# The down projection of the sample as seven block products, with its weight sums made by accumulating DRAM transfers in the gates' stage

## The chip, the cores and the metric

The kernel runs on one core of one Trainium2 chip. Its engines work in parallel, each through its own queue of instructions: TensorE (PE, with its weight loads PEld) multiplies matrices into PSUM; VectorE (DVE) and ScalarE (ACT) do elementwise work and copy results out of PSUM; GpSimd (POOL) does some elementwise work and issues part of the transfers; SyncE (SP) issues the rest. An engine takes its queue in order: an instruction that waits holds up all that stand behind it on that engine. The metric is the device time of the whole program in microseconds (us), smaller is better.

## The reference

One layer of a hybrid backbone works on 128 prompt tokens and 512 sample tokens with D = 1024 features, all in 32-bit floats. Mixers with gates and an output projection come first; behind them stands the feed-forward part, which matters here:

```python
def conv_ffn(h, w_up, cw, cb, w_down):
    z = dwconv3(h @ w_up, cw, cb)
    a, g = jnp.split(z, 2, axis=-1)
    return (jax.nn.silu(g) * a) @ w_down

    # in trunk_layer
    h = rmsnorm(x, lw['norm2_g']) * (1.0 + sc2) + sh2
    x = x + g2 * conv_ffn(h, lw['w_up'], lw['ffn_conv_w'], lw['ffn_conv_b'], lw['w_down'])
    # at the end, for the prompt and for the sample
    y = rmsnorm(x, final_norm_g)
```

`w_down` is 2816 x 1024. `g2` is the last of six modulation vectors: the product of silu(c) with 1024 columns of `w_ada`, one for the sample and one for the prompt.

## The kernel before, in words

All large products run in a split form. A 32-bit operand is cut into a high part, which TensorE takes in its fast 32-bit format, and a low part, the rest; a product is high x high + high x low + low x high, three matmuls. The high part is a copy on ScalarE (line 311 for weights, line 1774 for rows), the low part a subtraction on DVE (lines 312 and 1777). So each operand of a product costs both engines a pass.

The program is a list of `units`, one weight tile each with three steps: a load, a split ("prep"), and the matmuls. `ahead(i)` issues the loads of up to four units ahead (`DMA_AHEAD`) and the splits of up to two ahead (`PREP_AHEAD`). Side jobs (generators) are woken by `tick(us)`, which the matmul loops call with planned times; `start` puts such a job on the list and `drain` runs the jobs until something is there. A planner of the language then orders each engine's instructions by its own estimate of what is ready, except those pinned with `keep_in_program_order`; in the gates' and the up projection's stage all of DVE's, ScalarE's and POOL's (`ovec`, `oact`, `opool`) are pinned. Buffers are named regions of SBUF (`region("A", ...)`), used again and again: a region's next writer waits until its last reader is done. `rp` holds three raw weight tiles, `wp` three split ones. PSUM has eight banks, four in pairs (`pg`) and four single (`pm`).

The stages and their place in the profile:

- Up to about 300 us: norm, input projections and mixers, with the first gate tiles.
- 300 to 530 us: the gates (`g_pair`, matmuls at line 1124, branch products at line 1137). Tiles go in 14 pairs, and each pair is computed with seven block products in place of eight, Strassen's scheme in Winograd's form: sums of weight blocks (`g_sums`, DVE) and of operands take the place of one product. Weights come from `w_gp`, two loads of 640 KB per pair (line 1061), a pair ahead. POOL issues one load of branch operands in the third pair and one in the seventh (line 1174).
- 530 to 600 us: output projection (line 1264), second norm. POOL loads x for it (line 1253).
- 600 to 868 us: the up projection (`up_pair`, 22 pairs, matmuls at line 1480), also by seven products; the convolution's taps, the gate and `keep`, which writes one finished tile of 128 features x 641 tokens into the DRAM tensor `actd`, issued by POOL. Its columns are the 512 sample tokens, one pad and the 128 prompt tokens.
- 868 us to the end: the down projection (matmuls at line 1815). This is the stage that is changed.

In the down stage before, the output columns go in two halves `nh` of 512; for each, 11 units of two k (`kk_`, 128 features each) pass. `down_prep` splits the weight tile (128x1024: two k of 512 columns) and two activation tiles of 640 tokens, which `back` has loaded from `actd`. `down_tile` runs, for five row tiles t of 128 tokens (four of the sample, one of the prompt) and two k, three matmuls with the activation as the stationary 128x128 operand and 512 weight columns moving. In the second half the last three units are done together, row tile by row tile, and the prompt's tile is cut into two halves of 256 columns at the very end. `down_out` then multiplies a tile by `g2` (`gained`), adds it to x (`added`), squares and sums it for the norm (ScalarE), multiplies the first half by the norm's weight on POOL, and `down_store` scales and stores it.

Beside this `ada_cols` computes the eight 128-column pieces of `g2` (f = 40 to 47): DVE passes twice over a 128x1024 tile of `w_adt` per piece (line 263). It begins when the up projection is over, and `gain_rows` and `gain_load` turn the result into rows, which the first `down_out` needs.

Of the kernel before, what the change touches and what calls it, by code (L numbers as in the profile page):

```python
# [20 lines left out]
NPAIR = 22  # L21
BRIDGE = 4
# [46 lines left out]
def tile_step(ctx: ExitStack, tc: tile.TileContext, a: dict, outs: list, dbg=None):  # L69
# [168 lines left out]
    def ada_cols(fs, tag, homes, gap, last):  # L238
# [4 lines left out]
        act(cf, cf, AF.Silu)  # L243
# [9 lines left out]
        for f in fs:  # L253
            load(f + 1)
            if f in COLWAIT:
                yield COLWAIT[f]
# [32 lines left out]
    def gain_rows(i):  # L289

        m = pm()
# [664 lines left out]
    hdr = dram.tile([2, 2, P, 4, HC], F32, name="hdr")  # L956

# [382 lines left out]
    actd = dram.tile([NPAIR, P, T + 1], F32, name="actd")  # L1340
# [226 lines left out]
    def keep(p_):  # L1567
        opool.dma_start(actd[p_], up[p_, "z", 1])
# [11 lines left out]
    def up_pair(p_, r):  # L1580
# [30 lines left out]
        elif p_ == NPAIR - 1:  # L1611
            rd[UP + 1] = units[UP + 1][1](ld[UP + 1])
# [4 lines left out]
        if inner:  # L1617
            if p_ + 2 < NPAIR:
                r[p_ + 2] = up_load(p_ + 2)
            elif p_ + 2 == NPAIR:  # L1620
                fx["a01"] = rp.tile([P, 2, T], F32, tag="raw", name=nm("raw"))
                back(fx["a01"], 0, 2)
# [68 lines left out]
    def up_all(_):  # L1691
# [23 lines left out]
        def down_home():  # L1715
            if "col" not in fx:
                fx["col"] = region("X1", [P, 2560])
            return fx["col"][:, 0:D]

        start(ada_cols(range(40, 48), "MG1", lambda f: region("H", [P, D]) if f % 2 else down_home(), 3, 4))  # L1720
# [4 lines left out]
    ag = {}  # L1725
    AGT = ["E", "C", "A", "B", "D"]

    def actk(nh, k):
        if k < 2:
            if nh == 0:  # L1730
                return fx["a01"][:, k]
            if "fn" not in fx:
                fx["fn"] = region("F", [P, 2560])
                back(fx["fn"][:, 0:2 * T].rearrange("p (n t) -> p n t", n=2), 0, 2)
                nc.sync.dma_start(fx["fn"][:, 1280:2304], a["final_norm_g"].partition_broadcast(P))
            return fx["fn"][:, k * T:(k + 1) * T]
        i = (k - 2) // 4
        if i not in ag:
            ag[i] = region(AGT[i], [P, 4, T])
            back(ag[i], 2 + 4 * i, 6 + 4 * i)  # L1740
        return ag[i][:, (k - 2) % 4, :]

    def back(dst, n0, n1):
        src = actd[n0:n1].rearrange("n p t -> p n t")
        nc.sync.dma_start(dst[:, :, 0:TS], src[:, :, 0:TS])
        nc.sync.dma_start(dst[:, :, TS:T], src[:, :, TS + 1:T + 1])


    acc = {}
    x2v = {}  # L1750

# [6 lines left out]

    st3 = const.tile([P, 24], F32, name="st3")

    def down_prep(nh, kk_, pr):
        w = pr()
        if "s" not in fx:
            s_ = region("XH", [P, 4, 2, T], F32R)
            fx["s"] = [s_[:, j] for j in range(4)]
            for i in range(2):
                s_ = region("XL%d" % i, [P, 2, 2, T], F32R)
                fx["s"] += [s_[:, j] for j in range(2)]
        sl = []
        for k in (2 * kk_, 2 * kk_ + 1):  # L1770
            i = (nh * NFF + k) % 8
            s = fx["s"][i]
            hl = [s[:, 0, :], s[:, 1, :]]
            high = act(hl[0], actk(nh, k), AF.Copy)  # L1774
            if nh == 0 and kk_ in (1, 2):
                tc.keep_in_program_order(high)
            vec.tensor_tensor(hl[1], actk(nh, k), hl[0].bitcast(F32), ALU.subtract)
            sl.append(hl)
        return w, sl
# [443 lines left out]
```

## Time and profile before

| | |
|---|---|
| median of three runs | 1022.85 us (1022.79 to 1023.98) |
| span of the profiled execution | 1020.8 us; the page gives no other time for it, so 2.05 us of the median lie around the span |
| TensorE busy | 1008.7 us, 99% |
| DVE, ScalarE, POOL busy | 789.7 us, 538.4 us, 106.1 us |
| DMA | 177.85 MB, 174 GB/s in the mean |
| matmuls of the down stage | 678, from 853.8 to 1013.6 us |
| loads of `w_down` | 22 of 512 KB, 4.2 us to landing in the median |
| writes of `actd` by POOL | 22 of 320.5 KB, 5.5 us to landing |

The rows of the profile read as follows. A group's row gives line, engine, operation, the output and input tiles by name with their shapes, the count, then after the bar the busy time, the mean in ns and the idle time ahead of it with what ended it. A row of windows gives the window, its length, the busy time (and count) of PE, PEld, DVE, ACT and POOL, the granted clock as a share of full speed, the DMA share and GB/s. A row of a timeline or of the chain begins with the start in us and the duration. Matmuls overlap, so the distance from one to the next, not the row's mean, is what one costs. Lines 149 and such are a helper's, behind which many operations stand.

### The profile page before, as it was taken

Reading aid. Unit: us, or ns where it says so; the run is one execution under the profiler, and the core shown is the slowest. Engines: PE = TensorE matmul, PEld = TensorE weight load, DVE = VectorE, ACT = ScalarE, POOL = GpSimd, SP = SyncE. Lnnn points to the kernel's source line nnn. Section 1 sums busy time; section 2 is a strip of 40 time slices with the busy share of each in tenths; the row PEclk is TensorE's granted clock in tenths of the full one; section 3 lists DMA queues with packets and bytes.
Section 4 is the critical chain, followed back from the end, with each engine's and each line's share of the span. In section 5 each row is a group of like instructions: output and inputs, shape, how many; then the busy total and the mean of one; then the engine's idle time right before and its main releaser. Section 6 shows DMA issues by size and latency. Waiting matters only on the chain.

```text
span 1020.8 us, 18766 instructions
## 1 busy us (share of the span) xinstructions
PE 1008.7 (99%) x7572; PEld 953.0 (93%) x7572; DVE 789.7 (77%) x1308; ACT 538.4 (53%) x933; POOL 106.1 (10%) x153
## 2 busy tenths in 40 slices
PE   8999999999999999999999999999999999999997
PEld 6899999999999999999998899999999999888886
DVE  6759899779857676776868879988888887797644
ACT  6642343354545454444544567777777776633432
POOL 1000020322100000000010111111122211001101
PEclk9999999999999999999999999999999999999999
DMA  9864333697562413323288585755555669974212
GB/s 355 322 217 130 126 117 116 168 284 226 120 207 79 155 58 104 136 66 104 61 283 337 212 325 121 198 151 150 150 151 151 157 161 274 363 249 157 83 42 103
DMA packets 55926, 177.85 MB, mean 174 GB/s; under 512 B 8192, under 2 KB 14624, under 8 KB 53280
## 3 DMA queue, kind: packets, MB, share of 16 engines
q1 hardware_dynamic: 45008, 140.60, 40.2%
q0 software_dynamic: 10832, 36.06, 14.7%
q8 instruction: 59, 0.97, 0.4%
q14 instruction: 27, 0.22, 0.1%
HBM read 134.93 MB, written 25.46 MB: 157 GB/s over the span
## 4 chain that ended last, share of the span: by engine, by line
PE 92%; DVE 4%; DMA 2%; ACT 1%; issue 1%; SPq 0%; POOLq 0%; POOL 0%; DVEq 0%; ACTq 0%
PE g L1480 20%; PE m L1124 17%; PE g L363 14%; PE g L1815 8%; PE m L1815 6%; PE g L1137 5%; PE m L1480 4%; PE m L1264 3%; PE g L935 2%; PE g L1264 2%; PE m L149 2%; PE g L149 1%; PE m L1475 1%; PE m L527 1%; DMA A<-in_w_ada_dram 1%
## 5 line engine op out<-in xcount | busy, mean ns | idle before, releaser
L363 PE MATMUL g<-XH,w 128*128 128x320 f32 x704 | 171.0, 317 | 0.1
L363 PEld LDWEIGHTS g<-XH,w 128*128 128x128 f32 x704 | 120.6, 188 | 2.5 <-issue 1.0
L363 PE MATMUL g<-XL,w 128*128 128x320 f32 x352 | 108.7, 309 | 0.0
L363 PEld LDWEIGHTS g<-XL,w 128*128 128x128 f32 x352 | 66.3, 188 | 0.1
L312 DVE TENSOR_TENSOR w<-raw,w 128x1024 fp32r<-128x1024 f32 x34 | 41.5, 1221 | 14.7 <-ACT w L311 9.0
L1124 PE MATMUL m<-XH,w 128*128 128x320 f32 x224 | 52.5, 309 | 0.0
L1815 PE MATMUL g<-w,XH 128*128 128x512 f32 (+1 forms) x216 | 50.2, 385 | 0.0
L1815 PEld LDWEIGHTS g<-w,XH 128*128 128x128 f32 x216 | 39.5, 188 | 8.3 <-ACT XH L1774 0.3
L311 ACT ACTIVATE w<-raw 128x1024 fp32r<-128x1024 f32 x34 | 35.7, 1049 | 21.4 <-PE g L1264 9.9
L1815 PE MATMUL g<-w,XL 128*128 128x512 f32 (+1 forms) x180 | 42.5, 387 | 0.0
L149 DVE SCALAR_TENSOR_TENSOR X<-MG,p2t,X 128x641 f32<-128x641 f32 x44 | 38.9, 884 | 4.3 <-ACT X L149 3.4
L149 DVE SCALAR_TENSOR_TENSOR X<-X,p2t,X 128x641 f32<-128x641 f32 x44 | 38.8, 883 | 1.9 <-ACT X L149 1.0
L1815 PEld LDWEIGHTS g<-w,XL 128*128 128x128 f32 x180 | 33.4, 188 | 7.4 <-DVE dt L1830 0.7
L149 ACT ACTIVATE w<-raw 128x1024 fp32r<-128x1024 f32 (+3 forms) x46 | 38.5, 852 | 2.5 <-DMA raw<-in_w_in_dram 1.4
L1480 PE MATMUL g<-XL,w 128*128 128x320 f32 x240 | 38.6, 310 | 0.0
L1480 PE MATMUL g<-XL,C 128*128 128x320 f32 x240 | 38.4, 309 | 0.0
L1124 PEld LDWEIGHTS m<-XH,w 128*128 128x128 f32 x224 | 38.2, 188 | 0.0
L1480 PEld LDWEIGHTS g<-XL,w 128*128 128x128 f32 x240 | 36.0, 188 | 0.5 <-ACT MG L149 0.3
L1815 PE MATMUL m<-w,XH 128*128 128x512 f32 (+1 forms) x156 | 36.4, 381 | 0.0
L1480 PEld LDWEIGHTS g<-XL,C 128*128 128x128 f32 x240 | 36.0, 188 | 0.4 <-ACT MG L149 0.4
L1124 PE MATMUL m<-XL,w 128*128 128x320 f32 x112 | 34.6, 309 | 0.0
L1815 PEld LDWEIGHTS m<-w,XH 128*128 128x128 f32 x156 | 28.5, 188 | 5.6
(549 smaller groups left out, 2749.8 us busy)
## 6 DMA issues: line engine op xcount, KB each, us to landing
raw<-in_w_up_dram SPq DMA_DIRECT2D x30, 512.0 KB, 5.0
raw<-in_w_gp_dram SPq DMA_DIRECT2D x21, 640.0 KB, 3.9
raw<-in_w_down_dram SPq DMA_DIRECT2D x22, 512.0 KB, 4.2
raw<-in_w_in_dram SPq DMA_DIRECT2D x19, 512.0 KB, 4.3
H<-in_w_adt_dram SPq DMA_DIRECT2D x16, 512.0 KB, 4.2
actd<-X POOLq DMA_DIRECT2D x22, 320.5 KB, 5.5
X<-in_w_adt_dram SPq DMA_DIRECT2D x10, 512.0 KB, 4.3
upd<-XL SPq DMA_DIRECT2D x4, 1280.0 KB, 6.5
```

Of the source, the lines that this page charges most:

```text
L149: r = f(*args, **kw)
L311: act(w[0], raw, AF.Copy)
L312: vec.tensor_tensor(w[1], raw, w[0].bitcast(F32), ALU.subtract)
L363: mm(o, w[:, h, k0 + k, :], r(k)[:, s], start=(k == 0 and i == 0), stop=(k == kt - 1 and i == 2))
L527: mm(m[W * g:W * g + W, (i - s0) * W:(i - s0 + 1) * W], lhs, rhs, start=True, stop=True, tile_position=(64 * par, W * g))
L935: mm(o, x(kx)[:, ts], w[:, h, k, :], start=(kx == 0 and i == 0), stop=(kx == 7 and i == 2))
L1124: mm(o, w[:, k, :], x[:, k, :], start=(first and k == 0 and j == 0), stop=(k == 3 and j == 2), skip_group_check=True)
L1137: mm(pb[:, c, 0:HC], w[:, h + k, :], y[:, x, k, s], start=(k == 0 and j == 0), stop=(k == 1 and j == 2))
L1264: mm(m, mh[k // 2][:, hx, k % 2, t * P:(t + 1) * P], wo[q][:, hw, k % 2, :], start=(k == 0 and i == 0), stop=(k == 7 and i == 2))
L1475: mm(o, w[:, k, :], x[:, k, :], start=(first and not part and k == 0 and j == 0), stop=(part == 1 and k == 3), skip_group_check=True)
L1480: z = mm(o, w[:, k, :], x[:, k, :], start=(first and k == 0 and j == 0), stop=(k == 3 and j == 2), skip_group_check=True)
L1815: mm(ps, sl[k][hx][:, t * P:(t + 1) * P], w[:, hw, k, c0:c1], start=first, stop=end and (last or nh == 1 and t == 4 and kk_ == 7))
```

## The change: what it does

The sample's product (512 tokens x 2816 features by 2816 x 1024) is cut in two in each direction: tokens c = 0, 1 (256 each), features h = 0, 1 (11 tiles of 128 each, `NK`), output columns n = 0, 1 (512 each). The eight block products become seven, in sequence (`PHASES`; the prediction calls them blocks 1 to 7): p = 1, 5, 6, 2, 7, 4, 3. Each has six units: five of two k and one of one k. The prompt's 128 rows keep the plain product: they go along as a third row tile in the four blocks p = 1, 5, 2, 3, and where the weight is a sum (p = 5) the part that is too much is subtracted again.

The weights of p = 5, 6, 7 and 4 are sums of blocks. `down_sums` makes them in DRAM (`wsum`) with 48 transfers of up to 512 KB, 24 plain copies and 24 that add to their destination. POOL issues four of them at the start of each pair of the gates' stage from the second pair on, pinned in its queue. The sums of the operands (p = 5, 6, 7 and 3) are DVE operations of 128x512 in place (`x_sum`), one per unit.

PSUM: the products are accumulated so that later ones add to the banks of earlier ones (`bank`); copies of some banks (`c1`, `u2`, `u3`, `cp`) are kept in SBUF by ScalarE. The upper left, lower right and prompt results are put together in block 6 (`LATER`: `out_22`, `out_11`) from a bank and a copy; POOL multiplies and adds the part of `u2` and `cp` (`taken`), six operations of 128x512. At the end of block 6 come the upper right quarters (`half_two`), and the lower left ones and the prompt's second half with block 7.

`keep` writes in two layouts, one for the sample (`actx`, by feature half and token half) and one for the prompt (`actp`), two transfers where there was one; `x_load` reads them back. The weight loads are 42 in place of 22. There are four w buffers and five raw ones. The pieces of `g2` go on with shorter pauses, from other buffers, and stand still for units 9 to 14 (`PAUSE`); the gain is fetched at unit 26 (`G2`). The first unit's split stands behind the last pair's products in `up_pair`, where it stood ahead of them. `w_down` is laid out on the host as four blocks (`w_dn`).

The diff, cut to its core:

```diff
@@ ada_cols
-        act(cf, cf, AF.Silu)
+        z = act(cf, cf, AF.Silu)
+        if fs[0] == 40:
+            tc.keep_in_program_order(z)
...
             load(f + 1)
+            while R.get("pause"):
+                yield 1
@@ before the gates
+    wsum = dram.tile([4, P, NK, 512], F32, name="wsum")
+    def down_sums():
+        b11, b21, b12, b22 = [a["w_dn"][i] for i in range(4)]
+        s = [wsum[i] for i in range(4)]
+        cuts = [slice(k, min(k + 2, NK)) for k in range(0, NK, 2)]
+        for pairs in (((s[0], b11, 0), (s[2], b22, 0)), ((s[0], b12, 1), (s[2], b12, 1)), ((s[1], s[0], 0),),
+                      ((s[1], b22, 1),), ((s[3], s[1], 0),), ((s[3], b21, 1),)):
+            for k in cuts:
+                for o, i, add in pairs:
+                    if add:
+                        opool.dma_start(o[:, k], i[:, k], accum_op=ALU.add, max_dma_last_dim=1024)
+                    else:
+                        opool.dma_start(o[:, k], i[:, k])
+                    yield
@@ g_all
+        sums_ = down_sums()
         for p_ in range(GPAIR + 1):
+            for _ in range(4 if p_ else 0):
+                next(sums_, None)
@@ keep
-        opool.dma_start(actd[p_], up[p_, "z", 1])
+        z, (h, k) = up[p_, "z", 1], divmod(p_, NK)
+        opool.dma_start(actx[h].rearrange("c p k t -> p c k t")[:, :, k], z[:, 0:TS].rearrange("p (c t) -> p c t", c=2))
+        opool.dma_start(actp[h][:, k], z[:, TS + 1:T + 1])
@@ up_pair
         elif p_ == NPAIR - 1:
-            rd[UP + 1] = units[UP + 1][1](ld[UP + 1])
+            x_load("E")
+            ld[UP + 2] = units[UP + 2][0]()
...
+        if p_ == NPAIR - 1:
+            x_load("C")
+            rd[UP + 1] = units[UP + 1][1](ld[UP + 1])
+            ld[UP + 3] = units[UP + 3][0]()
@@ up_all
-        start(ada_cols(range(40, 48), "MG1", lambda f: region("H", [P, D]) if f % 2 else down_home(), 3, 4))
+        start(ada_cols(range(40, 48), "S0", lambda f: region("H" if f % 2 else "G", [P, D]), 1, 1), 0)
@@ the down stage
+    KS = [(0, 1), (2, 3), (4, 5), (6, 7), (8, 9), (10,)]
+    PHASES = [(1, "w", 0, (0, 0), 0), (5, "s", 0, (0, 1), 0), (6, "s", 1, (0, 0), None), (2, "w", 1, (1, 0), 1),
+              (7, "s", 2, (0, 1), None), (4, "s", 3, (1, 1), None), (3, "w", 3, (1, 0), 1)]
+    DOWN = [(ph, j) for ph in range(7) for j in range(6)]
+    JOIN = {(4, 4), (5, 0), (6, 3), (6, 4)}
...
+    def x_sum(p_, ks):
+        x = lambda h, c: x_raw(h, c, ks)
+        if p_ == 5:
+            vec.tensor_tensor(x(0, 1), x(0, 1), x(1, 1), ALU.subtract)
+        elif p_ == 6:
+            vec.tensor_tensor(x(0, 0), x(0, 1), x(0, 0), ALU.subtract)
+        elif p_ == 7:
+            vec.scalar_tensor_tensor(x(0, 1), x(0, 0), -1.0, x(1, 1), ALU.mult, ALU.subtract)
+        elif p_ == 3:
+            vec.tensor_tensor(x(1, 0), x(1, 0), x(0, 0), ALU.add)
...
+        x_sum(p_, ks)
+        act(w[:, 0, 0:n], raw, AF.Copy)
+        for o, i, r in ((0, 256, x_raw(h, c, ks)),) + (((256, 384, xr["p", hp][:, ks[0]:ks[-1] + 1]),) if hp is not None else ()):
+            act(s[:, 0, 0:n, o:i], r, AF.Copy)
+            vec.tensor_tensor(s[:, 1, 0:n, o:i], r, s[:, 0, 0:n, o:i].bitcast(F32), ALU.subtract)
+        vec.tensor_tensor(w[:, 1, 0:n], raw, w[:, 0, 0:n].bitcast(F32), ALU.subtract)
...
+    def bank(p_, t):
+        if t == 4:
+            return acc["p" if p_ in (1, 2) else "q"]
+        return acc["b3" if p_ == 2 else "b2" if p_ in (5, 3) else "b1"][t]
...
+    def taken(nh, t, x, op):
+        pool.tensor_tensor(x, x, grows["g2"][:, 0 if t < 4 else 1, nh * 512:nh * 512 + 512], ALU.mult)
+        xs = x2[t][:, nh * 512:nh * 512 + 512]
+        pool.tensor_tensor(xs, xs, x, op)
+
+    def half_one(nh, t):
+        xs = x2[t][:, nh * 512:nh * 512 + 512]
+        q = st3[:, t:t + 1]
+        act(prods[t], xs, AF.Square, accum_out=q)
+        pool.tensor_tensor(xs, xs, xr["F"][:, nh * 512:nh * 512 + 512], ALU.mult)
+        vec.tensor_scalar(q, q, 1.0 / D, EPS, ALU.mult, ALU.add)
+
+    def down_out(p_, t, c0, c1, ps):
+        if p_ == 5 and t == 4:
+            vec.tensor_tensor(acc["cp"], ps, acc["cp"], ALU.subtract)
+        elif p_ in (1, 6):
+            act(acc["cp"] if t == 4 else acc["c1" if p_ == 1 else "u2"][t], ps, AF.Copy)
+        elif p_ == 7:
+            act(acc["u3"][t], ps, AF.Copy)
+        elif p_ == 4:
+            half_two(0, t + 2, 0, 512, ps)
+        elif p_ == 3:
+            half_two(1, t, c0, c1, ps)
+
+    def joined(nh, t, ps, x, op):
+        y = gp.tile([P, 512], F32, tag="gt", name=nm("y"))
+        vec.tensor_tensor(y, ps, x, op)
+        gained(nh, t, 0, 512, y)
+        added(nh, t, 0, 512)
+        half_one(nh, t)
...
+    LATER = {(5, 1): (lambda: out_22(0),), (5, 3): (lambda: out_22(1),), (5, 2): (lambda: out_11(0),),
+             (5, 4): (lambda: out_11(1),), (5, 5): (lambda: out_11(4),)}
```

More of the change, by code (lines that the diff above doesn't have):

```diff
@@ L21 @@
 NPAIR = 22
+NK = NPAIR // 2
 BRIDGE = 4
@@ L1757, in x2r @@
         return x2v[tag]
-    st3 = const.tile([P, 24], F32, name="st3")
[L1761 to L1779, printed above, removed]
@@ L1799, in down_tile @@
[L1799 to L1807 removed]
+            x2[4] = x2r("G")[:, 0:1024]
+            r = region("H", [P, 2, 512])
+            acc["u3"] = [r[:, 0], r[:, 1]]
+        for f in LATER.get((ph, j), ()):
+            f()
+    def bank(p_, t):
+        if t == 4:
+            return acc["p" if p_ in (1, 2) else "q"]
+        return acc["b3" if p_ == 2 else "b2" if p_ in (5, 3) else "b1"][t]
@@ L1808, in down_tile @@
+    def down_tile(u, ws):
+        ph, j = DOWN[u]
+        p_, _, _, _, hp = PHASES[ph]
+        down_start(u)
+        hold.append((KS[j], ws))
+        if (ph, j) in JOIN:
+            return
+        batch = hold[:]
+        hold.clear()
+        end = j == 5
+        for t in (0, 1, 4) if hp is not None else (0, 1):
+            halved = p_ == 3 and t == 4 and end
             for ci, (c0, c1) in enumerate(((0, 256), (256, 512)) if halved else ((0, 512),)):
-                ps = (acc["halves"][ci] if halved else acc[nh][t])[:, 0:c1 - c0]
```

210 lines of the change are left out of this document (120 added, 90 removed).

## The prediction

> **What bounds the kernel now.** I read the page's busy shares and its chain of waits first, then windows by stage, then the tables of groups for the last stage alone, and the timeline where two engines meet.
>
> ```profile
> span 1020.8 us, 18766 instructions
> PE 1008.7 (99%) x7572; PEld 953.0 (93%) x7572; DVE 789.7 (77%) x1308; ACT 538.4 (53%) x933; POOL 106.1 (10%) x153
> PE 92%; DVE 4%; DMA 2%; ACT 1%; issue 1%; SPq 0%; POOLq 0%; POOL 0%; DVEq 0%; ACTq 0%
> ```
> ```profile
> 424.00:439.80 15.80, 15.80 (x109) 15.80 (x109) 11.32 (x19) 7.27 (x13) 0.00 (x0) 1.00 0.25 83
> 750.00:800.00 50.00, 50.00 (x343) 50.00 (x342) 44.38 (x65) 35.66 (x62) 9.21 (x12) 1.00 0.60 153
> 900.00:925.00 25.00, 25.00 (x112) 20.67 (x112) 23.33 (x38) 8.29 (x11) 0.00 (x0) 1.00 0.69 233
> 975.00:1000.00 25.00, 25.00 (x112) 20.65 (x111) 10.25 (x13) 6.53 (x9) 0.14 (x1) 1.00 0.07 22
> ```
>
> TensorE never stops in these windows (columns: window, its length, then busy time of PE, PEld, DVE, ACT and POOL, clock, DMA share, GB/s). In the gates (first row) DVE has 4.5 us to spare in each 15.8 and DMA three quarters; in the up projection DVE is at 89%; in the down stage it is at 93% while the last gain columns run and at 41% afterwards. So removed matmul time is time, as long as DVE can feed the shorter stage.
>
> **The matmuls removed.** One row per form, the down stage alone, and the beat of the chain:
>
> ```profile
> L1815 PE MATMUL g<-w,XH 128*128 128x512 f32 x204 | 48.6, 391 | 0.0
> L1815 PE MATMUL g<-w,XL 128*128 128x512 f32 x174 | 41.6, 390 | 0.0
> L1815 PE MATMUL m<-w,XH 128*128 128x512 f32 x144 | 34.8, 389 | 0.0
> L1815 PE MATMUL m<-w,XL 128*128 128x512 f32 x120 | 29.3, 389 | 0.0
> ```
> ```profile
> 877.09 5.44 PE g L1815 x24
> ```
> ```profile
> 1011.60 0.88 PE L1815 MATMUL m<-w,XL 128*128 128x256 f32 x6
> 1012.32 1.60 PE L1815 MATMUL m<-w,XH 128*128 128x256 f32 x12
> ```
>
> 204 + 174 + 144 + 120 = 642 matmuls of 512 columns; the code has 36 more of 256. The beat is 5.44/24 = 0.2267 us, and (1012.32 - 1011.60)/6 = 0.12 us for a half. Before: 642 x 0.2267 + 36 x 0.12 = 149.9 us. After: the sample takes 7 products x 11 k x 2 row tiles x 3 = 462; the prompt, which keeps the plain product, takes 11 x 3 in each of three blocks and, in the last, 18 whole and 30 half ones. That is 579 x 0.2267 + 30 x 0.12 = 134.9 us. **TensorE saves 15.0 us.** Operand shapes stay, so the beat stays.
>
> **What the stage asks of DVE.** The table of groups from 868 us on gives the durations:
>
> ```profile
> L312 DVE TENSOR_TENSOR w<-raw,w 128x1024 fp32r<-128x1024 f32 x20 | 24.4, 1220 | 3.5 <-ACT w L311 3.0
> L1834 DVE TENSOR_TENSOR G<-G,dt 128x512 f32<-128x512 f32 x2 | 1.4, 685 | 0.0
> L1834 DVE TENSOR_TENSOR G<-G,dt 128x256 f32<-128x256 f32 x2 | 0.8, 424 | 0.0
> L1777 DVE TENSOR_TENSOR XH<-E,XH 128x640 fp32r<-128x640 f32 x4 | 3.1, 820 | 4.1 <-ACT XH L1774 4.1
> L1830 DVE TENSOR_TENSOR dt<-g,S 128x512 f32<-128x512 f32 x6 | 4.1, 690 | 6.6 <-PE g L1815 4.6 <-DMA S<-growd 2.0
> L1877 DVE SCALAR_TENSOR_TENSOR X<-X,st,F 128x512 f32<-128x512 f32 x4 | 3.0, 750 | 2.0 <-POOL st L1871 2.0
> L263 DVE SCALAR_TENSOR_TENSOR junk<-H,MG 128x1024 bf16<-128x1024 f32 x4 | 4.9, 1220 | 1.6 <-DMA H<-in_w_adt_dram 1.6
> ```
>
> Neighbours overlap by some 0.08 us, so I count 1.14, 0.61 and 0.35 us for 1024, 512 and 256 columns, and 0.73 where one operation needs the last one's result. Low parts of a unit of two k: weights 1.14, sample rows 0.61, prompt rows 0.35 (four blocks), a sum of operands 0.61 (four blocks). A unit needs:
> - block 1: 2.10 us of DVE against 4.08 of PE (18 matmuls)
> - block 2: 2.71 against 4.08; block 4: 2.10 against 4.08; block 7: 2.71 against 4.08
> - blocks 3 and 5: 2.36 against 2.72 (12 matmuls); block 6: 1.75 against 2.72
>
> The gain columns take two passes of 1.22 us each and some 0.2 for the rest, about 2.6 us, eight times. They run in blocks 1 and 2, stop for units 9 to 14, and end in block 4; blocks 1 and 2 need 5.5 x (2.10 + 2.71) = 26.5 of DVE beside some 17 for six or seven columns, 43.5 of 45 us. That just fits, with weight loads five deep over it. ScalarE, busy 8.3 of 25 us in that window now, has room.
>
> Block 6 is where it does not fit. There the results of four quarters and of the prompt are put together: four joins of three dependent operations (0.73 + 0.73 + 0.61 + 0.15 = 2.2 us), one of 1.5 for the prompt, and after its end two final quarters (0.73 + 0.61 + 0.15 + 0.75 = 2.25 each). From its start to the last low part, with the first two units prepared ahead, DVE has: 3 x 1.75 + 0.95 for units 3 to 6 of the block, 5 x 2.71 + 1.5 for block 7, 8.8 + 1.5 + 4.5 for results, 1.3 for a prompt quarter: 37.3 us. PE has 14.96 + 22.6 us in these two blocks, and the last unit must be ready 7.7 us before the end (its first use comes 10.4 us of matmuls before the end, 2.7 us after that batch's start), which leaves 29.9. DVE can run ahead some 3 us (the w buffers are four, and the first joins read banks that are long done). **Short by 4.4 us**, which PE waits.
>
> **POOL against DVE.** The change adds six POOL multiplications and additions of 128x512 to the five that are there now, all in block 6. This is what one does to DVE now:
>
> ```profile
> L1845 POOL TENSOR_TENSOR X<-X,F 128x512 f32<-128x512 f32 x4 | 5.9, 1485 | 64.2 <-ACT dt L1844 64.2
> ```
> ```profile
> 945.16 1.21 DVE L312 TENSOR_TENSOR w<-raw,w 128x1024 fp32r<-128x1024 f32 x1
> 946.36 1.86 DVE L1777 TENSOR_TENSOR XL<-C,XL 128x640 fp32r<-128x640 f32 x1
> 948.20 2.58 DVE L1777 TENSOR_TENSOR XL<-C,XL 128x640 fp32r<-128x640 f32 x2
> 943.12 1.51 DVE L1834 TENSOR_TENSOR X<-X,dt 128x512 f32<-128x512 f32 x1
> 938.58 0.15 DVE L1846 TENSOR_SCALAR st<-st 128x1 f32<-128x1 f32 x1 [0.79 <-ACT dt L1844]
> 945.47 2.07 POOL L1845 TENSOR_TENSOR X<-X,F 128x512 f32<-128x512 f32 x1 [1.39 <-ACT dt L1844]
> ```
>
> The DVE operation ends at 948.2 instead of 947.2: 1.86 us where the same shape takes 0.82, and POOL's own took 2.07. Three of DVE's were held so (the 1.51 us at 943.12 for 0.68, and one of the pair at 948.20, 2.58 us for 1.55), 2.9 us together for five POOL operations. Eleven would cost 11 x 2.9/5 = 6.4 us; none is the lower end, if DVE happens to read PSUM meanwhile. I take 3, since joins are half PSUM reads and the last POOL operations fall behind the shortage. The stall is then 7.4 us.
>
> The Trainium skill, "SBUF — State Buffer", "Who interferes with whom", says that a VectorE instruction with two SBUF inputs and a GpSimd instruction that reads SBUF share a port and one holds it for its whole length. The rows above agree; taken at its full strength the rule is the second rival below.
>
> **The weight sums in the gates.** 48 transfers of up to 512 KB (23 MB), four per pair from the second pair on. Rows:
>
> ```profile
> L1061 SPq DMA_DIRECT2D raw<-in_w_gp_dram x21: 327/328/383, 267.1 to 475.9; - x21
> DMA to landing us min/median/max: 3.7/3.9/6.2
> 396.73 16.17 SPq L1061 DMA_DIRECT2D raw<-in_w_gp_dram  x3
> 415.89 0.33 SPq L1061 DMA_DIRECT2D G<-in_w_gp_dram  x1
> 421.89 1.35 ACT L149 ACTIVATE w<-raw 128x1024 fp32r<-128x1024 f32 x2
> 343.32 0.57 POOL L1174 DMA_DIRECT2D E<-ybd  x1 [56.82 <-PE g L1137]
> 406.68 0.55 POOL L1174 DMA_DIRECT2D A<-ycd  x1 [62.79 <-PE g L1137]
> 512.61 0.54 POOL L1253 DMA_DIRECT2D G<-in_x_prompt_dram  x1 [105.38 <-DVE D L149]
> L149 POOL DMA_DIRECT2D actd<-X x22 | 18.3, 832 | 19.6 <-DVE X L149 19.6
> q0 software_dynamic: 10832, 36.06, 14.7%
> w<-raw POOLq DMA_DIRECT2D x6, 512.0 KB, 8.2
> ```
>
> POOL has no work there, and nothing paces it but two loads of branch operands (at 343.3 and 406.7 us, both waiting for PE), so the transfers go out in three bursts, of 8, 16 and 24, each beside a few pairs. Queue 0 now moves 36.06 MB in 14.7% of the span, 240 GB/s, so 23 MB are 96 us of transfer time in some 200. An accumulating one has two reads, for which only the 8.2 us of 512 KB into SBUF stand: the last 24 at 8.2 each would run to 406.7 + 197 us and hold back the five loads of x that POOL issues from 512.6 on; at 4 us each they end at 505. They overlap, so I take the shorter. The two weight loads of a pair go out at 412.6 (the last of the three merged in the row) and 415.9 and are first read at 421.9 and, one long split later, 423: 9 and 7 us, of which the landing takes 3.9. ScalarE is busy 7.3 of the pair's 15.8 us, so a late start is partly made up. They may take some 7 to 10 us. I take 0.5 us for this, bounds 0 and 24 (third rival). By "DMA: Bandwidth & Descriptors", "Queues, rings and completion order", in the Trainium skill, engines take queues in turn by packets, by which 3.9 us becomes at most 7.8, and the 0.5 us and the third rival would fall away.
>
> **Small parts.** `keep` issues two transfers instead of one: 22 more of 0.83 us on POOL, which is busy 9.2 of 50 us in that stage; the buffer that they read is written again more than a pair (84 matmuls, 12 us at the windows' 343 in 50) later. SP issues 42 weight loads instead of 22 and waits for the last `keep` before a tail load; five raw buffers cover that. The first unit's split now stands behind pair 21's products instead of ahead of them, so PE has less to fill the end of the up projection with; Silu of the two vectors is pinned on ScalarE behind a 1 MB load. I take 1 us, bounds 0 and 4. The tail keeps its form: two halves of the prompt last.
>
> **Sum.** 1020.8 - 15.0 + 7.4 + 0.5 + 1.0 = 1014.7 us of span; the median of the runs lies 2.05 us above the span, so 1016.8.
>
> **Rivals.**
> 1. *DVE keeps up* (joins and low parts interleave so that PE waits under 3 us). For it: DVE at 93% cost PE nothing from 900 to 925. Against: the 37.3 us above. 1022.85 - 15.0 + 1.5 + 1 = 1010.4.
> 2. *POOL and DVE exclude each other throughout* (slower). If each POOL operation stops DVE for its own 1.28 to 1.49 us, and joins wait for ScalarE's squares as one does for 0.79 us now, block 6 loses 11 x 1.4 = 15 us more: 4.4 + 15 + 1.5, so 1022.85 - 15.0 + 20.9 = 1028.8. It decides from a stall of 13.5 us on. For it: the held operations above waited about as long as POOL's ran. Against: five POOL operations cost DVE only 2.9 us now.
> 3. *The sums hold back the gates' loads.* If a load lands 3 us after its latest time in eight pairs, 24 us in place of the 0.5: 1040.3. For it: a load took 6.2 us where DMA was near full. Against: the 10 us it may take.
> 4. *The saving goes at the borders*, where a bank waits for the copy of its last block: six borders at the 0.8 us that a wait for ScalarE takes above, 5 us on top: 1021.8, no change that can be told.
>
> **Chances.** Mine 0.50, rivals 0.18, 0.17, 0.09 and 0.06. What a measurement can tell is 0.2%, 2 us. Faster: nearly all of the first two, 0.65; same, the edges of mine and the last, 0.12; slower 0.23. Mine alone spans 1012 to 1021; with rival 1 and the near part of rival 2 the range is 1009 to 1028.
>
> **What would show it.** The beat of 0.2267 us with 609 matmuls in the down line; PE without a gap through the first five blocks and gaps released by DVE (low parts of w) in the last two, 4 to 12 us together; DVE over 95% busy there, with 512-column operations of 1.3 us and more beside POOL; pairs of 15.84 us unchanged in the gates. Wrong if the gates' pairs lengthen, if gaps come in the first two blocks (loads or gain columns), or if block 6 runs through.

## The result, and the profile after

The changed kernel takes 1021.82 us (median; 1018.16 to 1025.61), the kernel before, measured beside it, 1022.69 us (1021.96 to 1023.98). The ratio is 0.999, with a 95% interval of 0.9981 to 0.9999: a gain of 0.9 us, where 6 were forecast and 15 us of matmul time were taken out. The profiled execution took 1023.17 us, 1.4 us above the median, with a span of 1021.4 us, so its rows add up to somewhat more than the change loses in the median. The span of before stood 1.9 us under its median, this one 0.4 us, so the two spans, set side by side, make the change look 1.5 us worse than it is.

The page of the changed kernel, its span, busy shares and chain:

```profile
span 1021.4 us, 18956 instructions
PE 997.7 (98%) x7503; PEld 942.7 (92%) x7503; DVE 828.5 (81%) x1379; ACT 559.8 (55%) x982; POOL 182.6 (18%) x229
PE 84%; DVE 8%; DMA 3%; issue 2%; ACT 2%; POOL 0%; SPq 0%; POOLq 0%; DVEq 0%; ACTq 0%
```

PE fell from 92% of the chain to 84%; VectorE and the transfers took its place. The windows of the down stage (window, length, busy time of PE, PEld, DVE, ACT, POOL, the granted clock, the DMA share, GB/s) show where:

```profile
859.60:875.00 15.40, 12.19 (x56) 10.48 (x55) 10.31 (x18) 8.77 (x15) 1.27 (x2) 0.89 0.89 332
875.00:900.00 25.00, 21.80 (x95) 17.39 (x95) 21.11 (x37) 13.62 (x21) 1.27 (x2) 1.00 0.78 274
900.00:925.00 25.00, 25.00 (x105) 20.47 (x104) 24.02 (x40) 12.19 (x20) 0.00 (x0) 0.93 0.93 334
925.00:950.00 25.00, 25.00 (x112) 20.49 (x111) 25.00 (x43) 14.61 (x25) 2.78 (x1) 1.00 0.75 251
950.00:975.00 25.00, 23.98 (x106) 19.50 (x105) 24.96 (x28) 15.01 (x22) 14.17 (x6) 1.00 0.46 144
975.00:1000.00 25.00, 21.79 (x95) 17.40 (x94) 24.51 (x37) 16.36 (x33) 8.48 (x7) 1.00 0.35 111
```

PE, which before lost 0.03 us of the 75 from 925 to 1000, is short of 25 us in the first two rows and in the last two. In 900 to 925 it is busy throughout and still starts 105 matmuls where 112 fit: the clock column says 0.93. VectorE (the third number), 41% busy in the last window of before, is at 98 to 100% in the last three. What PE waited for from 858 us on:

```profile
PE m L1901 <- DVE MG L1845: 4.2, 2, 3.2
PE g L1901 <- ACT XH L1843: 3.2, 1, 3.2
PE m L1901 <- DVE w L1845: 1.8, 1, 1.8
PE g L1901 <- DVE dt L1916: 1.4, 1, 1.4
```

Two waits of 3.2 us are the early ones; the other three, 1.0 (the rest of the first row), 1.4 and 1.8, are the late ones, 4.2 us together. ScalarE and VectorE are only the last to arrive in the early ones. The chain names what they waited for themselves:

```profile
856.72 8.52 DMA C<-actp
891.79 4.07 DMA H<-in_w_adt_dram
```

and SP's queue in the timeline, with the `keep` transfer of GpSimd's queue last, shows why these two were late:

```profile
855.78 0.33 SPq L1775 DMA_DIRECT2D F<-in_final_norm_g_dram  x1
856.16 0.44 SPq L1781 DMA_DIRECT2D A<-actx  x1
856.72 0.38 SPq L1769 DMA_DIRECT2D C<-actp  x1
...
891.38 0.32 SPq L1788 DMA_DIRECT2D C<-actx  x1
891.79 0.38 SPq L252 DMA_DIRECT2D H<-in_w_adt_dram  x1
```
```profile
883.64 0.71 POOL L150 DMA_DIRECT2D actx<-X  x1 [14.35 <-DVE X L150]
```

```profile
895.89 1.23 DVE L268 SCALAR_TENSOR_TENSOR junk<-H,S 128x1024 bf16<-128x1024 f32 x1 [3.89 <-DMA H<-in_w_adt_dram]
```

The last row is VectorE's. The prompt's rows (C from `actp`), which the third row tile of the very first unit needs, went out behind 512 KB of norm gains that nothing needs for 100 us and 640 KB of block two's rows, and took 8.52 us to land. The second place is the tail load of `x_tail(1, 1)`: it must wait for the last `keep`, issued at 883.64 and landed 7.7 us later, and went out at 891.38. SP's queue stood still for 8 us, and behind the tail load stood that of gain column H. VectorE works in the order written, so it waited 3.89 us for that column with low parts of weights, already loaded, behind it.

A third loss shows in the clock alone, in windows cut where it falls and where it rises again:

```profile
865.79:869.20 3.41, 3.41 (x11) 3.13 (x12) 3.35 (x8) 3.25 (x5) 1.18 (x2) 0.50 0.75 294
899.92:903.33 3.41, 3.41 (x10) 2.63 (x9) 3.41 (x6) 0.63 (x1) 0.00 (x0) 0.50 0.96 344
```

The gaps end at 865.7 and 898.65. Behind each of them PE runs at half its clock for 3.41 us, from 0.1 us behind the first gap on and from 1.3 us behind the second. That costs 3.41 x 0.50 = 1.7 us each time. By these rows the two early places cost 3.2 + 1.7 + 3.2 + 1.7 = 9.8 us, the late waits 4.2.

### The profile page after: what moved, and what is told of

It reads as the page before. It is cut to its first block, busy times and chain, and to the rows that moved or that the text cites. A ratio compares the mean times of both kernels' runs of the same rounds, so it can differ in the third digit from the quotient of the medians.

```text
span 1021.4 us, 18956 instructions
## 1 busy us (share of the span) xinstructions
PE 997.7 (98%) x7503; PEld 942.7 (92%) x7503; DVE 828.5 (81%) x1379; ACT 559.8 (55%) x982; POOL 182.6 (18%) x229
## 4 chain that ended last, share of the span: by engine, by line
PE 84%; DVE 8%; DMA 3%; issue 2%; ACT 2%; POOL 0%; SPq 0%; POOLq 0%; DVEq 0%; ACTq 0%
PE g L1505 19%; PE m L1145 17%; PE g L368 14%; PE g L1158 5%; PE m L1505 4%; PE m L1901 4%; PE m L1288 3%; PE g L1901 3%; PE g L940 2%; PE g L1288 2%; PE m L150 2%; PE g L150 1%; PE m L1500 1%; PE m L532 1%; DVE w L1845 1%
## 5 line engine op out<-in xcount | busy, mean ns | idle before, releaser
L1901 PE MATMUL m<-w,XH 128*128 128x512 f32 (+1 forms) x330 | 77.3, 384 | 1.9 <-DVE w L1845 1.8
L1901 PEld LDWEIGHTS m<-w,XH 128*128 128x128 f32 x330 | 60.6, 188 | 14.8 <-DVE w L1845 2.7
L150 POOL DMA_DIRECT2D wsum<-in_w_dn_dram x36 | 36.5, 1160 | 54.0 <-issue 42.2
L1901 PE MATMUL g<-w,XH 128*128 128x512 f32 x141 | 35.3, 396 | 4.6 <-ACT XH L1843 3.2
L1901 PEld LDWEIGHTS g<-w,XH 128*128 128x128 f32 x141 | 26.6, 190 | 10.8 <-ACT XH L1843 3.6
L150 ACT ACTIVATE ga<-m,cst 128x320 f32<-128x320 f32 x27 | 14.3, 528 | 36.3 <-PE m L1145 36.3
L329 ACT ACTIVATE w<-raw 128x1024 fp32r<-128x1024 f32 (+1 forms) x22 | 24.3, 1103 | 16.1 <-issue 6.6
L150 DVE TENSOR_TENSOR w<-raw,w 128x1024 fp32r<-128x1024 f32 (+2 forms) x36 | 30.7, 872 | 2.2 <-ACT w L150 2.1
```

The source lines that it names most:

```text
L150: r = f(*args, **kw)
L329: high = lambda: act(w[:, 0], raw, AF.Copy)
L1901: mm(ps, s[:, hx, k, o:o + P], w[:, hw, k, c0:c1], start=first, stop=i == 2 and bi == len(batch) - 1 and k == len(ks) - 1, skip_group_chec ...
```

## The experiments

The theory at this point: the 15 us are real, and 10 of them go to the order of SP's queue (theory A). Its rivals were that those waits are only a symptom of a stage in which VectorE lacks time anyway (theory C), and that GpSimd is what makes VectorE late at the end. All times are medians; ratios are to the kernel before, measured beside each group (1022.68, 1022.79 and 1022.74 us).

**The prompt's rows first.** `issue_after` puts a transfer behind the one named, on its queue.

```diff
-            nc.sync.dma_start(xr["p", 0], actp[0])
+            xr["go"] = nc.sync.dma_start(xr["p", 0], actp[0]).ins
...
-            nc.sync.dma_start(xr["F"][:, 0:D], a["final_norm_g"].partition_broadcast(P))
+            with tc.issue_after(xr["go"]):
+                nc.sync.dma_start(xr["F"][:, 0:D], a["final_norm_g"].partition_broadcast(P))
```

The same is done to the loads of A, B and D, of column 40 and of unit 5's weights.

> Only the order of transfers on SP's queue changes: the prompt's rows of half one are issued ahead of the 512 KB of norm gains, the 640 KB of block two and the gain columns. Theory A (the first gap on PE, 3.37 us, and the half clock behind it, about 1.5 us, come from where this transfer stands in the queue, 8.52 us from issue to landing): it lands in 5 to 6 us, the gap shrinks to under 0.7 us, the clock stays at 1, and the time falls by 3.5 to 5 us against the changed kernel, to about 1017.5 us. Theory B (the transfer is late because its buffer comes free only at 855.9 us, and the rows of weights take the bandwidth in any order): under 1 us of gain. Theory C (what is won early is given back to VectorE in the last three blocks): the gap goes, but the time falls by under 1.5 us.

1016.4 us, ratio 0.9941 (0.9929 to 0.9954): 5.4 us faster than the changed kernel. The chain at that place:

```profile
855.08 5.11 DMA C<-actp
```

It lands in 5.1 us in place of 8.5, at 860.2 and not at 865.2, and the matmuls run on. So theory A holds for the first gap, and B falls. The gain is above the range because the second gap shrank too, to 1.12 us, and the clock stayed at 1.00 behind it: with the up projection's last products done 5 us sooner, the last `keep` went out at 877.27 in place of 883.64, and the load of column H, behind the tail load that waits for it, at 883.89 in place of 891.79. C holds in part: PE now waits 1.55 us for a column at 932 and 1.20 us for low parts at 956, which it did not before.

**The waiting tail load later.**

```diff
-            if part == 1:
+            if part == 1 and tag != "B":
                 x_tail(h, c)
...
+        if u == 7:
+            x_tail(1, 1)
```

> The one tail load that waits for the last kept rows of the activation is issued with unit 7 of the stage and not with unit 2, so that nothing stands behind it in SP's queue while it waits. Theory A (the second gap, 3.34 us at 895.08, is VectorE waiting in its order for a gain column whose load stood behind that tail load, and the clock is granted low behind it for about 1.9 us): the H column loads are issued 8 us earlier, the gap goes, and the time falls by 4.5 to 5.5 us, to about 1017 us. Theory C (given back in the last three blocks, where VectorE is 98 to 100% busy): under 1.5 us. Theory D (the clock drop behind the gap is the throttle's own and not the gap's): the gap goes but the granted clock in 898 to 906 stays at 0.7 to 0.8, and the gain is 3.3 us.

1018.6 us, ratio 0.9963 (0.9949 to 0.9976): 3.2 us faster. PE's wait at this place:

```profile
894.52 2.79 PE L1903 MATMUL m<-MG,MG 128*128 128x512 f32 x11 [1.13 <-DVE MG L1845]
```

1.13 us remain of 3.18, and the clock of 892 to 906 is 1.00 throughout, which ends theory D. The loss had two parts: 2 us of the queue and, as the clock is only lowered behind the long gap, 1.7 us of that. The remaining 1.1 us were VectorE's own; the size in A, 4.5 us and more, was too high by that. PE's wait for the prompt's rows, which this edit does not touch, is 2.20 us in this execution and 3.21 in that of the changed kernel: single executions differ by that much.

**Both.**

> Both edits of queue order at once. Theory A: they add, 8.5 to 10.5 us against the changed kernel, about 1011.5 to 1013.3 us; what is left over the beat of 0.2267 us per 512 columns is the 4 to 5 us of gaps in the last three blocks. Theory C (VectorE's work in the second half of the stage sets the end, whatever is won early): under 4 us together, and the gaps of the last three blocks grow by what was won.

1014.35 us, ratio 0.9919 (0.9905 to 0.9932): 7.5 us faster than the changed kernel, where the single gains add to 8.6. That is below A's 8.5 and far above C's 4: the queue's order did cost most of what the rows said, but not all of it comes back. The waits of PE and four windows of this run:

```profile
PE m L1916 <- DVE w L1858: 3.5, 2, 1.8
PE g L1916 <- DVE dt L1931: 1.1, 1, 1.1
PE g L301 <- DVE gcol L278: 0.6, 1, 0.6
```
```profile
860.00:880.00 20.00, 19.73 (x96) 16.63 (x95) 19.52 (x34) 15.19 (x26) 2.55 (x4) 1.00 0.97 356
880.00:900.00 20.00, 20.00 (x90) 16.55 (x89) 20.00 (x36) 9.49 (x16) 0.00 (x0) 1.00 0.91 311
900.00:920.00 20.00, 20.00 (x90) 16.57 (x89) 19.49 (x33) 11.96 (x20) 0.00 (x0) 1.00 0.98 367
920.00:940.00 20.00, 19.43 (x86) 15.54 (x85) 20.00 (x36) 10.99 (x19) 0.00 (x0) 1.00 0.78 252
```

Nothing but VectorE is waited for now, and it is busy for 79.0 of 80 us from the stage's start on. PE's waits, 0.6 us at 929 and 1.7, 1.1 and 1.8 from 952 on, are 5.2 us in place of the changed kernel's 4.2 late ones, and in this execution the clock falls to half once more behind the last. That is the C that was left, and the next runs take it up.

**GpSimd's six operations left out**, on top of both edits:

```diff
     def taken(nh, t, x, op):
-        pool.tensor_tensor(x, x, grows["g2"][:, 0 if t < 4 else 1, nh * 512:nh * 512 + 512], ALU.mult)
-        xs = x2[t][:, nh * 512:nh * 512 + 512]
-        pool.tensor_tensor(xs, xs, x, op)
+        pass
```

> As the run with both edits, and the six operations of GpSimd that add the first and sixth block's part to the second output half (taken) are left out: the second half of the first 256 rows and of the prompt lacks those terms. Theory A (GpSimd's operations stretch VectorE's beside them, 6.5 us of VectorE's time in the sixth of the blocks and before it): against the run with both edits the gaps of the last three blocks shrink by 2 to 3.5 us, and VectorE's operations of 1.4 to 2.3 us are back at 0.4 to 1.2 us. Theory E (these gaps are VectorE's own work, or banks that come free late, and GpSimd is harmless): within 0.7 us of the run with both edits.

1013.31 us, ratio 0.9907 (0.9893 to 0.992): 1.0 us faster than with them, between the two ranges; the intervals of the two runs overlap, so the size is not sure. In the changed kernel these rows stand beside each other:

```profile
953.89 0.70 DVE L1844 TENSOR_TENSOR XH<-A,XH 128x512 fp32r<-128x512 f32 x1
954.59 1.44 DVE L1844 TENSOR_TENSOR XH<-F,XH 128x256 fp32r<-128x256 f32 x1
955.95 1.78 DVE L1824 TENSOR_TENSOR D<-D,E 128x512 f32<-128x512 f32 x1
959.09 2.31 DVE L1845 TENSOR_TENSOR w<-raw,w 128x1024 fp32r<-128x1024 f32 x1
```
```profile
947.22 8.53 POOL L1923 TENSOR_TENSOR XL<-XL,S 128x512 f32<-128x512 f32 x1 [62.30 <-DMA S<-growd]
957.14 3.17 POOL L1925 TENSOR_TENSOR X<-X,XL 128x512 f32<-128x512 f32 x2
```

At first GpSimd is the one that is held: its first operation takes 8.53 us, with VectorE's beside it at 0.70. From 954.6 on VectorE's are stretched: 256 columns take 1.44 us in place of 0.43, 512 take 1.78 in place of 0.70, 1024 take 2.31 in place of 1.23, 1.0 to 1.1 us more each, whatever the length. The stretching is as strong as theory A has it; its price is one wait. In the run with both edits the six operations run from 940.0 to 950.3, and PE waits right behind them:

```profile
953.61 2.79 PE L1916 MATMUL m<-w,XH 128*128 128x512 f32 x11 [1.66 <-DVE w L1858]
```

Without them this wait is gone, and the one for `gcol` is 1.1 us in place of 0.6. The late gaps stay: 1.9 us for `w`, 0.9 for `dt`. The Trainium skill, "SBUF — State Buffer", "Who interferes with whom", describes the shared port; the rows agree, and the time it costs depends on where the operations fall.

**The weight sums left out**, on top of both edits: `down_load` reads `w_dn[i]` in the place of `wsum[i]`, and `g_all` does not call `down_sums`.

> As the run with both queue edits (1014.35 us), with the accumulating transfers of the gates' stage left out; the down stage reads the plain weight blocks in the place of their sums, so that the sample's output is that of other weights at the same cost in the stage. Theory A (the 60 transfers, 10 to 12 us each for 512 KB, are hidden: PE's last matmul of the gates came 0.5 us later with them): 0 to 0.7 us faster. Theory F (the DMA engines, busy for 92 to 109% of two windows of the gates' stage, hold its loads, and the down stage hides that by waiting less): 1.5 us or more.

1014.6 us, ratio 0.992 (0.9907 to 0.9933), against 1014.35 with them. (The code issues 48 such transfers, not 60; 24 of them add.) The same window of the gates, first with the sums (the changed kernel), then without:

```profile
407.00:470.00 63.00, 63.00 (x432) 63.00 (x431) 45.44 (x68) 28.71 (x53) 21.91 (x25) 1.00 1.09 286
```
```profile
407.00:470.00 63.00, 63.00 (x432) 63.00 (x431) 45.09 (x69) 28.70 (x52) 0.01 (x1) 1.00 0.32 105
```

432 matmuls in 63.00 us both times, with a DMA share of 1.09 and of 0.32. The sums are hidden altogether; F falls.

**Gain columns in the up projection.** With both edits in, the eight columns are worked out by a job of their own in the up projection, one column at a time from region H, and `gain_rows` is called where the last of them was waited for, at unit 26:

```diff
-        start(ada_cols(range(40, 48), "S0", lambda f: region("H" if f % 2 else "G", [P, D]), 1, 1), 0)
+        drain(lambda: "early_cols" in R)
...
+            if p_ == 5:
+                start(early_cols(range(40, 48), 24), 0)
             up_pair(p_, r)
...
-            drain(lambda: "ada47" in R)
+            gain_rows(1)
```

> As the run with both queue edits, and all eight gain columns (16 operations of 1.22 us and their small ones, some 22 us of VectorE's time) are worked out in the up projection's stage, one column every second pair, in place of blocks one to four of the down stage. Theory G (with the two waits gone, VectorE, 20.0 of 20 us busy in nearly every window from 858 to 980, sets the down stage's 8.7 us over PE's beat): the gaps of the stage fall to 2 to 4 us and the time to 1008 to 1011 us. Theory H (VectorE is as short in the up projection, 88 to 93% busy): PE gaps of the same size come up there, and the time stays within 1 us of 1014.35 or above.

1022.95 us, ratio 0.9999 (0.9989 to 1.001). Both theories were wrong. H is: PE's busy time in 600 to 858 us is what it was, 257.31 us against 257.30 with the columns in their old place. G's prediction failed for another reason:

```profile
967.74 0.69 DVE L1953 TENSOR_TENSOR dt<-y,S 128x512 f32<-128x512 f32 x1 [1.93 <-DMA S<-growd]
968.35 1.79 DVE L1879 TENSOR_TENSOR XH<-B,XH 128x512 fp32r<-128x512 f32 x1
```
```profile
967.80 3.49 POOL L1960 TENSOR_TENSOR XL<-XL,S 128x512 f32<-128x512 f32 x2 [86.04 <-ACT H L1977]
```

The gain rows came only with unit 26, and both engines needed them at 967.7. VectorE waited for them with units' low parts behind it, and then worked beside all six of GpSimd's operations, at 1.79 us for 0.69. PE waits 5.1 us for `w` in the stage and 1.8 for `dt`. By these rows it matters where GpSimd's work falls, but this run has the wait for the rows in it as well and does not part the two. Some 2 us of this execution were lost at 253 to 261 us, long ahead of the stages that the edit is about; the later runs with such a job do not show it.

> As the run before, with four of the eight columns moved and four left in the down stage. Theory G: half of the effect, 1011 to 1012.5 us. Theory H: within 1 us of 1014.35.

With four columns moved, `early_cols(range(40, 44), 40)`, and the gain rows fetched at unit 24 in place of 26, the rest as in the run with both edits: 1012.46 us, ratio 0.99 (0.9887 to 0.9913), 1.9 us faster than 1014.35 and as G has it. The intervals overlap a little; the trace is clearer. Of PE's four waits in the run with both edits, those for `gcol` and at 952 are gone, and 1.8 us for `w` and 0.9 for `dt` are left. How much of it is the columns and how much the earlier rows is not shown.

**Low parts by transfer.** For units 20, 22, 24 and so on to 34:

```diff
+        if u in LOWS:
+            act(w[:, 1, 0:n], w[:, 0, 0:n].bitcast(F32), AF.Copy, scale=-1.0)
+            pool.dma_start(w[:, 1, 0:n], raw, accum_op=ALU.add)
...
-        vec.tensor_tensor(w[:, 1, 0:n], raw, w[:, 0, 0:n].bitcast(F32), ALU.subtract)
+        if u not in LOWS:
+            vec.tensor_tensor(w[:, 1, 0:n], raw, w[:, 0, 0:n].bitcast(F32), ALU.subtract)
```

> As the run with both queue edits, and for eight units of blocks four to six the low part of the weights is not subtracted on VectorE (8 times 1.22 us) but made by ScalarE (a negated copy) and an accumulating transfer from GpSimd's queue, as the up projection does for two of its parts. Theory G (VectorE's time sets the gaps): 2 to 4 us faster than 1014.35. Theory I (the transfer of 512 KB is late for the matmul, or stands behind GpSimd's six operations on the second half, which wait for their banks): PE waits for w by DMA, and the time is 1 to 6 us above 1014.35.

1022.83 us, ratio 1.0004 (0.9992 to 1.0017), 8.5 us slower than without: theory I, and worse than its range. PE waits for such transfers in five places, 11.8 us together. One wait is 6.75 us, with PE at half its clock from 959.05 to 965.87, and GpSimd's queue before it explains it:

```profile
946.30 2.75 POOL L1943 TENSOR_TENSOR XL<-XL,S 128x512 f32<-128x512 f32 x2 [5.09 <-DMA S<-growd]
...
954.49 1.59 POOL L1945 TENSOR_TENSOR G<-G,XL 128x512 f32<-128x512 f32 x1
956.03 0.88 POOL L1857 DMA_DIRECT2D w<-raw  x1
```
```profile
960.64 5.06 PE L1921 MATMUL m<-w,XH 128*128 128x512 f32 x11 [6.75 <-DMA w<-raw]
```

The accumulating transfer stood behind the six operations and went out at 956.03, when PE was already waiting. This settles nothing on VectorE's share; it shows the price of a queue that carries both.

**Columns and rows early.** As the run with all columns moved, the columns a little faster (a gap of 19 in place of 24), and the rows with units 14 and 16:

```diff
+        if u == 14:
+            gain_rows(1)
...
+        if u == 16:
+            grows["g2"] = gain_load(1, "S0")
```

> As the run with all columns in the up projection's stage (1022.95 us), but the columns come a little faster, so that none falls into the last pair, and the gain rows made of them are written and read back with units 14 and 16 of the stage and not with unit 26. Theory J (that run lost because VectorE waited 1.93 us at 965.8 for the gain rows and GpSimd's six operations, released by the same rows, all ran at 967.8 to 979 beside VectorE's, each of which took twice its time): those gaps, some 8 us, go, and the time is 1008 to 1012 us. Theory H (VectorE's time in the up projection is what is missing): PE gaps there, and over 1016 us.

The x rows of the prompt (`x2[4]`) are fetched at unit 14 as well. 1010.86 us, ratio 0.9889 (0.9872 to 0.9905), 12.1 us faster than the run that it mends. Theory J holds, though the edits in it were not run apart. Two waits of PE are left in the stage:

```profile
PE m L1941 <- DVE w L1880: 1.9, 1, 1.9
PE g L1941 <- DVE dt L1956: 1.1, 1, 1.1
```

**Outputs a block sooner.**

```diff
-    LATER = {(5, 1): (lambda: out_22(0),), (5, 3): (lambda: out_22(1),), (5, 2): (lambda: out_11(0),),
-             (5, 4): (lambda: out_11(1),), (5, 5): (lambda: out_11(4),)}
+    LATER = {(4, 1): (lambda: out_11(0),), (4, 3): (lambda: out_11(1),), (4, 5): (lambda: out_11(4),),
+             (5, 1): (lambda: out_22(0),), (5, 3): (lambda: out_22(1),)}
```

> As the run before, and the three outputs of block three's group (out_11) are worked out one block sooner, with units 25, 27 and 29 in place of 32, 34 and 35. Theory K (the gap of about 1.0 to 1.5 us before the seventh block is PE waiting for the bank that shares its pair with the one still being read, and VectorE is idle in 900 to 960): this gap goes and the three blocks' VectorE work is spread, 1 to 2.5 us faster than the run before. Theory L (these operations only stand ahead of the units' preparations in VectorE's order and hold them): 0 to 3 us slower.

1007.77 us, ratio 0.9857 (0.9842 to 0.9872), 3.1 us under the run before it, 15.0 us under the kernel before and 14 under the change as it was made: the version to keep. No wait of PE is left in the down stage. Two windows of its blocks five and six:

```profile
940.00:960.00 20.00, 20.00 (x90) 16.57 (x89) 18.77 (x26) 12.43 (x21) 3.50 (x2) 1.00 0.64 185
960.00:980.00 20.00, 20.00 (x89) 16.33 (x88) 19.96 (x29) 13.99 (x24) 5.92 (x3) 1.00 0.47 146
```

VectorE is at 94 and 100% and PE waits for nothing: full it may be, as long as the order suits. Both late waits went with this one edit, more than theory K asked. The one for `dt` is, by the code, a shared pair of banks: `out_11(4)` reads `p`, and block seven's prompt starts in `q`, the other half of the same tile; with `p` read a block sooner the wait is gone.

> As the run with half of the columns moved (1012.46 us), with the same three outputs one block sooner. Theory K: the gap of 1.03 us before the seventh block goes, 0.5 to 1.5 us faster, about 1011.3 us. Theory L: 1013 us or above.

1009.18 us, ratio 0.9866 (0.9851 to 0.988), 3.3 us faster than with half of the columns alone, again above K's range: the edit is worth the same in either place. L falls.

## Why the prediction was wrong

**PE's saving of 15.0 us: right.** The stage shows 609 matmuls, and the last version, in which PE waits for nothing, is 15.0 us faster than the kernel before.

**The gates' sums at 0.5 us: nothing was lost there, and the bound of 24 was far too wide.** A pair of the changed kernel's gates still takes 413.93 - 398.09 = 15.84 us:

```profile
398.09 1.76 PE g L1158 x12
...
413.93 1.76 PE g L1158 x12
```

The landing of their 28 loads went from 3.9 to 6.8 us in the median and from 6.2 to 12.5 at the longest, and PE never waited for one. By the rule of "DMA: Bandwidth & Descriptors" in the Trainium skill, "Queues, rings and completion order", as the prediction read it, they would stay under 7.8; the trace agrees in the median and not at the longest. The last 24 sums, which the prediction ends at 505 us (its own 406.7 + 24 x 4 makes 503), had landed by 473.

**The small parts at 1.0 us, bounds 0 and 4: the step that failed.** It named the right wait, SP's for the last `keep`, and closed it with "five raw buffers cover that". They cover the weights. What stood behind the waiting tail load was also the gain column's load, and behind that column, on VectorE, the low parts of weights that were already there. The same step listed the first unit's split but not the order in which the first unit's other operands leave SP's queue, by which the prompt's rows came third. And the end of a stall was taken as the end of its cost, where PE then ran at half its clock for 3.41 us. Together 9.8 us by the rows, 7.5 by the run that mends both.

**The columns in blocks one and two, "43.5 of 45 us, just fits", at no cost: right for these two blocks, not for what follows.** With the queue mended VectorE is at 97 to 100% up to 940 us, and PE's first wait comes at 929, in block four: 0.6 us for the columns, and 1.7 for low parts in block five. Both are gone in the run with four columns moved and the gain fetched sooner, 1.9 us faster.

**The stall of 7.4 us in block six: too high and in the wrong place.** PE waits 4.2 us in the last three blocks. The six additional operations of GpSimd were scheduled from 947 us on, in blocks four and five and not in block six, and cost about 1.0 us (the run without them), not the larger part of 3. The 1.4 us for `dt` are, by the code, a bank pair that the working had not looked at; the run with the outputs a block sooner, in which this wait is gone, fits that: VectorE's time is not short there, its order is.

Against the forecast span of 1014.7 us the profile has 1021.4, 6.7 more: 8.8 by the early places (9.8 for 1.0), less 3.2 for the late waits (4.2 for 7.4), less the 0.5 of the gates. Of the remaining 1.6 us, 0.5 were lost by 282 us, ahead of the first sum (286.7), and 0.4 behind the last matmul; 0.7 have no row.

Of the rivals, the fourth gave the right time (1021.8 us) by luck, for a wrong reason: of the six borders one shows a wait, the 1.4 us for `dt`. The third falls with the run without sums. The second falls: it asked for a stall of 13.5 us, PE waits 4.2 in those blocks, and six of the eleven operations left out gained 1.0. The first, VectorE keeping up at 1010.4 us, is what the kernel can do when the order suits, and 2.6 us better than it was priced. Of the signs, the beat, the load on VectorE and the stretched operations beside GpSimd were there; "wrong if gaps come in the first two blocks (loads or gain columns)" is what came.

## What to carry to other kernels

Write down the new order of every queue before pricing its pieces: for each transfer that waits, what stands behind it, and which engine, working in order, has ready work behind that. Count 1.7 us or more on top of a stall of PE of over 2 us, for the half clock that stood behind each of these here. When a bound engine is nearly full, moving its work to an earlier stage helps only if everything made from that work moves too.

## What the runs showed of the hardware

**A short stall halves PE's clock for 3.41 us.** Behind waits of 3.21 and 3.18 us the granted clock was 0.50 for 3.41 us each time, shown above. A wait of 2.20 us (the run with the tail later) was enough:

```profile
863.77:867.18 3.41, 3.41 (x12) 3.08 (x13) 3.35 (x8) 3.20 (x5) 1.23 (x2) 0.50 1.01 402
```

A wait of 1.8 to 1.9 us for low parts near the end is there in eight of the runs. In two of them (the run with both edits, and that without GpSimd's six operations) the clock fell to 0.50 for 3.41 us behind it; in the other six it stayed at 1.00, as it did behind the waits of 1.0 to 1.7 us. The Trainium skill, "TensorE: Matmul & The Clock Gate", "Part 1: The HAM clock gate", gives a window of about 3.4 us that runs freely, which would explain that the same wait costs once and not another time; that the stall itself can be clearly shorter than the window is what these runs add. The changed kernel's time goes with the clock: its 20 executions go from 1018.16 us at a mean clock of 0.999 to 1025.61 at 0.991, where the kernel before, beside the experiments, was always at 0.998 or 0.999.

**Transfers from DRAM to DRAM are slow, whether they add or copy, and cost PE nothing here.** The page's row for `wsum` from `w_dn` mixes both kinds. Apart, first eight plain copies (issued at 287 to 296 us), then six that add (361 to 378 us):

```profile
wsum<-in_w_dn_dram POOLq DMA_DIRECT2D x8, 512.0 KB, 14.6
wsum<-in_w_dn_dram POOLq DMA_DIRECT2D x6, 512.0 KB, 9.4
```

The plain loads of 640 KB beside them landed in 6.8 us in the median. An adding one took GpSimd 1.25 us to issue, a plain copy 0.52. The DMA share was 1.09 in the window of the gates shown above, and PE did not lose a matmul.
